# A threshold search that notes its passes in ten columns, and a scheduling clock with the trace's durations

## The chip, the cores and the metric

One core of a Trainium2 chip runs the whole program. The metric is device time in microseconds (us) of one execution. The engines named below are TensorE (PE, with its weight loads PEld), VectorE (DVE), ScalarE (ACT), GpSimd (POOL) and SyncE (SP), whose queue issues the DMAs. Each engine takes its instructions strictly in the order in which they stand in its list.

## The reference, cut to what matters

One layer of a streaming encoder runs for 2048 prompt frames and for 8 x 16 sample frames. After a common projection there are three head groups: A (causal attention with forget gates), B (attention over the best keys of an indexer) and C (attention over a band of chunks). The indexer part is what the change touches:

```python
rs = jax.nn.relu(jnp.einsum('bqhe,bke->bqhk', iq, ik) * IDX_SCALE)
score = jnp.einsum('bqh,bqhk->bqk', iw * IDX_W_SCALE, rs)
score = jnp.where(adm[None], score, -jnp.inf)
top_val, top_idx = lax.top_k(score, n_top)     # n_top = 256 for the prompt
# ... softmax attention of group B over the n_top keys of each query ...
y = x + jnp.einsum('bne,ed->bnd', g, w_out)    # g: the gated outputs of A, B and C
```

## The kernel before, in words

The work falls into streams of steps, written as Python generators: projections of the prompt (`fill_stream`, matmuls `pj<-wt,hT`), dense units of groups A and C (`maxima`, `rows`, `scores`, `products`, `end`), the indexer's scores and the choice of keys for query blocks i = 2 to 15 (`score_stream`, `select_stream`), the sample frames (`sample_stream`, tiles `yy`, `acc`, `cum`, `eq` of the selection used again), the sparse units of group B, and the output projection with the final norm (`out_stream`, matmuls `pj<-wo,gac`).

`drive` (L429) merges the streams into one program. A step says what it needs; `Clock` (L63) holds for every engine the time to which it has been given work, and for every tile when it will be ready, worked out from a cost in ns for each instruction (`Timed`, L181). `drive` gives the next piece to the stream whose need is met first; where no stream is ready, one of the fillers (projection or output matmuls) goes in. These costs therefore settle the order on PE, ACT, DVE and POOL, and nothing is reordered later. Two more decisions hang on them: `exp_split` (L514) puts the difference `Pl<-Pf` (the low half of the exponentials, which `o<-V,Pl` multiplies) on POOL or on DVE, whichever is expected free first, and every step that waits for a tile is put behind the work that is expected to be done by then.

The choice of keys, `select` (L1026), looks for a threshold with about 252 of n scores above it. A pass counts on ACT by a Sign activation over the whole row with a summed output (`eq<-acc,un`), and POOL computes from the sum the error `ee`, a changed slope `iv` (with `eg` and `hv`) and the next threshold `un`, with one element per partition. There are ten counts in a block. After `un`, POOL also keeps the best threshold so far and its count in `ub` and `eb`, with `ea` as the mark of a count that is too high. When all passes are done, DVE picks the exact set of 256 keys (among others with a prefix sum, `cum`), and the mask goes to memory as `negd`.

Three gates set the order far from the search. Block i + 1 is scored while block i is searched, since there are two `acc` tiles. `smp_stream` starts only when all 14 blocks are chosen. And `out_all` lets the output projection of the sample rows (block 16, `open_(b)` at L1987) start only when `smp_s` has ended; that is the last tile of the program.

`sample_stream` runs 24 heads, one after the other, as one list of steps: copies of the queries into `QM` (`acc<-qp`, `yy<-q`), 18 matmuls of scores, softmax on DVE and ACT, then for the head before it six transposes, four copies, 51 matmuls of products, the division on DVE, the gate on POOL, and a transpose by DMA.

A second program behind `tc.If(fv > FORCE)` is in the built lists too and is not run.

Of the kernel before, what the change touches and what calls it, by code (L numbers as in the profile page):

```python
# [10 lines left out]
F32 = mybir.dt.float32  # L11
F16 = mybir.dt.float16
BF16 = mybir.dt.bfloat16
# [22 lines left out]
TOP = 256.0  # L36
# [26 lines left out]
class Clock:  # L63
# [12 lines left out]
    @staticmethod  # L76
    def aps(args, kw):
        for x in (*args, *kw.values()):
            if hasattr(x, "tensor") and hasattr(x, "ap"):
                yield x  # L80

# [99 lines left out]
class Timed:  # L181
# [5 lines left out]
    def __getattr__(self, what):  # L187
# [3 lines left out]
        def call(*args, **kw):  # L191
# [14 lines left out]
            elif e == "DVE":  # L206
                if what == "scalar_tensor_tensor":
                    cost = (129 if ins[0].dtype == F32 and out[0].dtype == F32 and len(ins) > 2 else 68) + 1.042 * m
                elif what == "tensor_copy" and ins[0].dtype != F32:
                    cost = 68 + 0.26 * m if "ps" not in str(ins[0].tensor) else 68 + 0.52 * m  # L210
                elif what == "tensor_tensor_scan":
                    cost = 68 + 1.9 * m / 2
                else:
                    cost = 68 + 1.042 * m
            elif e == "ACT":
                cost = (52 if len(ins) == 1 else 142) + 0.836 * m + (60 if len(out) > 1 else 0)
            elif e == "POOL":
                if what == "memset":
                    cost = 40 + 0.83 * m
                elif m <= 8:  # L220
                    cost = {1: 240, 2: 260, 3: 320}.get(len(ins), 320) if what == "tensor_scalar" else 141
                else:
                    cost = 141 + 1.68 * m
# [34 lines left out]
def hybrid_step(ctx, tc, x_prompt, x_sample, cache_a_k, cache_a_v, cache_a_logf, cache_b_k, cache_b_v,  # L258
# [767 lines left out]
    def select(i, out):  # L1026
# [7 lines left out]
        def col(nm, w=1):  # L1034
            return sl.tile([128, w], F32, name=nm, bufs=2 if nm in ("ssg", "ee", "un") else 1)
# [7 lines left out]
        nmu, sa, u, iv, ub, eb = [col(k) for k in ("nmu", "sa", "u", "iv", "ub", "eb")]  # L1043
        yield need(acc, sx)
        V.reduce_sum(nmu, sx[:, :ng], axis=AX.X)
        yield need(nmu)
# [5 lines left out]
        kc = selc[:, i - 2, :]  # L1052
        G.tensor_scalar(u, kc[:, 0:1], sa, -1.0, op0=ALU.mult, op1=ALU.mult)
# [4 lines left out]
        yield need(u)  # L1058
        sums.append(sign(u))
        ep = None  # L1060
        for it in range(10):
            ss = sums.pop(0)
            yield need(ss)
            e, a = col("ee"), col("ea")
            G.tensor_scalar(e, ss, 0.5, n / 2 - TARGET, op0=ALU.mult, op1=ALU.add)
            if 0 < it < 9:
                if ep is not None:

                    g = col("eg")
                    G.tensor_scalar(g, e, ep, 0.0, op0=ALU.mult, op1=ALU.is_lt)  # L1070
                    G.tensor_scalar(iv, g, hv, iv, op0=ALU.mult, op1=ALU.add)
                ep = e
                un = col("un")
                G.tensor_scalar(un, e, iv, u, op0=ALU.mult, op1=ALU.add)
                hv = col("hv")
                G.tensor_scalar(hv, iv, -0.5, None, op0=ALU.mult)
            G.tensor_scalar(a, e, TOP - TARGET + 0.25, -1e30, op0=ALU.is_gt, op1=ALU.mult)
            if it == 0:
                G.tensor_tensor(ub, a, tiny, ALU.add)
                G.tensor_tensor(eb, a, e, ALU.add)  # L1080
                continue
            G.tensor_scalar(ub, a, u, ub, op0=ALU.add, op1=ALU.max)
            G.tensor_scalar(eb, a, e, eb, op0=ALU.add, op1=ALU.max)
            if it < 9:
                u = un
                yield need(u)
                sums.append(sign(u))
        t, m1, g, v, kk = [col(k) for k in ("tt", "m1", "gg", "vv", "kk")]
# [997 lines left out]
```

## Time and profile before

| | |
|---|---|
| median of 3 runs | 2681.66 us (2680.62 to 2687.39) |
| the profiled execution's own time | 2682.99 us |
| its span in the profile | 2681.1 us |
| busy: PE, DVE, ACT, POOL | 2403.7, 1821.8, 1383.8, 1226.5 us |
| granted TensorE clock, mean over the span | 0.972 of full speed |

The span is the time between the first and the last instruction of the profile; 1.9 us of the profiled execution lie outside it. All instructions that a helper of the scheduling clock records carry that helper's line, L192, in the profile, so groups are known by their tiles and not by their lines. A wait is idle time of an engine just before an instruction, put down to what came last.

### The profile page before, as it was taken

How to read it: one execution, taken by the hardware profiler on the slowest of the kernel's cores; microseconds unless marked ns; L12 is line 12 of the kernel's file. 1: busy time of each engine (PE TensorE's matmuls, PEld its weight loads, DVE VectorE, ACT ScalarE, POOL GpSimd, SP SyncE). 2: the span in 40 equal slices, each digit the busy share in tenths (PEclk: the TensorE clock that was granted, in tenths of full speed). 3: DMA queues.
4: the chain of work that ended last, by engine and by line, in shares of the span. 5: the costliest groups of instructions: out<-in, count | busy, mean ns of one | idle time of the engine just before them, and what ended most of it. 6: DMA issues, size and time to landing. Idle time of an engine off the chain costs nothing.

```text
span 2681.1 us, 69388 instructions
## 1 busy us (share of the span) xinstructions
PE 2403.7 (90%) x26754; PEld 1673.4 (62%) x26838; DVE 1821.8 (68%) x4865; ACT 1383.8 (52%) x2734; POOL 1226.5 (46%) x2115
## 2 busy tenths in 40 slices
PE   4997888888999899889899999957879999999998
PEld 4666666666676676667677787744546555555553
DVE  6434667788677787857857446658786676778743
ACT  6314556656665576575545344445555444443310
POOL 0014577766564375573624103426465555544300
PEclk8999999999999999999999999978899999999999
DMA  6255313233333332223354453373254333244542
GB/s 199 62 130 147 92 43 86 68 91 85 92 92 87 96 78 72 65 72 97 96 136 109 111 124 84 80 150 83 58 147 93 75 74 85 73 97 101 122 104 82
DMA packets 553190, 257.25 MB, mean 96 GB/s; under 512 B 376064, under 2 KB 541760, under 8 KB 552592
## 3 DMA queue, kind: packets, MB, share of 16 engines
q1 hardware_dynamic: 552848, 252.71, 37.7%
q8 instruction: 212, 3.47, 0.6%
q14 instruction: 130, 1.06, 0.1%
HBM read 160.37 MB, written 84.85 MB: 91 GB/s over the span
## 4 chain that ended last, share of the span: by engine, by line
PE 47%; DVE 17%; POOL 15%; issue 8%; DMA 7%; ACT 4%; SPq 1%; DVEq 0%; ACTq 0%; POOLq 0%
PE pj L192 29%; PE st L192 8%; PE o L192 5%; PE s L192 4%; POOL Pl L192 3%; DVE jk L192 3%; DVE acc L192 2%; POOL iv L192 2%; POOL un L192 2%; ACT eq L192 2%; DVE mx L192 2%; POOL eb L192 2%; POOL eg L192 1%; DVE cum L192 1%; POOL ub L192 1%
## 5 line engine op out<-in xcount | busy, mean ns | idle before, releaser
L192 POOL TENSOR_TENSOR Pl<-Pf 128x512 f16<-128x512 f32 (+3 forms) x653 | 657.4, 1017 | 584.5 <-ACT Pf L192 551.6
L192 PE MATMUL pj<-wt,hT 128*128 128x128 f16 (+1 forms) x8568 | 783.1, 244 | 5.1 <-DVE ev L192 4.0
L192 PEld LDWEIGHTS <-hT 128*128 128x128 f16 x8976 | 655.8, 98 | 126.8 <-issue 31.4
L192 ACT ACTIVATE Pf<-st,sh 128x512 f32<-128x512 f32 (+1 forms) x496 | 297.3, 612 | 284.4 <-DVE st L192 110.0
L192 PEld LDWEIGHTS <-Pf 128*128 128x128 bf16 x5472 | 315.1, 98 | 98.4 <-issue 11.2
L192 PE MATMUL pj<-hT,wt 128*128 128x512 f16 (+1 forms) x1440 | 297.1, 351 | 1.0 <-ACT yy L192 0.7
L192 PEld LDWEIGHTS <-Pl 128*128 128x128 f16 x2736 | 255.1, 99 | 53.6 <-POOL Pl L192 50.6
L192 PE MATMUL pj<-wo,gac 128*128 128x512 f16 x1224 | 284.6, 381 | 1.9 <-DVE xr L192 1.7
L192 DVE SCALAR_TENSOR_TENSOR acc<-rl,iws,acc 128x512 f32<-128x512 f32 (+3 forms) x266 | 202.3, 761 | 91.2 <-ACT rl L192 86.6
L192 ACT ACTIVATE Pf<-st,ncb 128x512 f32<-128x512 f32 (+1 forms) x320 | 192.9, 623 | 91.0 <-PE st L192 82.3
L192 PE MATMUL o<-V,Pl 128*128 128x65 f16 x1648 | 198.9, 194 | 45.3 <-POOL Pl L192 42.8
L192 DVE TENSOR_REDUCE mx<-s 128x1 f32<-128x512 f32 (+2 forms) x320 | 185.5, 603 | 75.4 <-PE s L192 73.5
L192 DVE CUSTOM_DVE_ANT_0 jk<-s,ng 128x512 bf16<-128x512 f32 (+3 forms) x304 | 188.6, 620 | 70.9 <-PE s L192 52.1
L192 ACT ACTIVATE rl<-s 128x512 f32<-128x512 f32 (+3 forms) x304 | 161.5, 543 | 136.0 <-PE s L192 72.4
L192 PE MATMUL o<-V,Pf 128*128 128x65 f16 x3296 | 219.2, 195 | 1.4 <-DVE u L192 0.8
L192 PEld LDWEIGHTS <-wt 128*128 128x128 f16 x1440 | 127.2, 99 | 127.5 <-issue 15.3
L192 PEld LDWEIGHTS <-gac 128*128 128x128 f16 x1224 | 116.8, 98 | 130.2 <-issue 5.0
L192 ACT ACTIVATE ev<-pj 128x512 f32<-128x512 f32 (+4 forms) x211 | 115.0, 545 | 148.3 <-PE pj L192 137.2
L192 ACT ACTIVATE eq<-acc,un 128x384 bf16<-128x384 f32 (+13 forms) x112 | 146.9, 1311 | 83.7 <-POOL un L192 83.3
L192 PE MATMUL st<-qp,Ka 128*128 128x512 f16 (+3 forms) x544 | 182.7, 338 | 6.5 <-ACT Pf L192 5.4
L192 PE MATMUL st<-Q,K 98*128 98x512 f16 (+3 forms) x544 | 183.4, 339 | 0.6 <-ACT Q L192 0.6
L192 DVE TENSOR_TENSOR Pl<-Pf 128x512 f16<-128x512 f32 (+3 forms) x163 | 105.6, 654 | 46.7 <-ACT Pf L192 44.9
(452 smaller groups left out, 4486.1 us busy)
## 6 DMA issues: line engine op xcount, KB each, us to landing
wst<-in_w_in SPq DMA_DIRECT2D x84, 256.0 KB
gac<-gTd SPq DMA_DIRECT2D x34, 384.0 KB
out<-ev SPq DMA_DIRECT2D x96, 128.0 KB
qTd<-ev SPq DMA_DIRECT2D x96, 128.0 KB
szd<-ev SPq DMA_DIRECT2D x96, 128.0 KB
qp<-qTd SPq DMA_DIRECT2D x96, 128.0 KB
out<-xr SPq DMA_DIRECT2D x17, 512.0 KB
xt<-in_x_prompt SPq DMA_DIRECT2D x16, 512.0 KB
```

Source lines behind the costliest of these rows:

```text
L192: r = f(*args, **kw)
```

## The change

Two things are changed. In `select`, the thresholds and the counts of the passes stand in ten columns of the tiles `us` and `es`, so that POOL only computes the error and the next threshold in a pass; the mark of counts that are too high (`am`) and the best threshold and count are taken once, at the end of a block, by five DVE instructions. And the costs of the scheduling clock are other numbers: small POOL instructions, the prefix sum, DVE and ACT instructions with a summed output, ACT instructions that read SBUF.

```diff
@@ Clock
+    @staticmethod
+    def psum(x):
+        return getattr(x.tensor, "space", DRAM) == PSUM
@@ Timed
             elif e == "DVE":
                 if what == "scalar_tensor_tensor":
-                    cost = (129 if ins[0].dtype == F32 and out[0].dtype == F32 and len(ins) > 2 else 68) + 1.042 * m
+                    cost = (129 if len(ins) > 2 else 68) + 1.042 * m
...
                 elif what == "tensor_tensor_scan":
-                    cost = 68 + 1.9 * m / 2
+                    cost = 130 + 2.09 * m
                 else:
-                    cost = 68 + 1.042 * m
+                    cost = 68 + 1.042 * m + (70 if kw.get("accum_out") is not None else 0)
             elif e == "ACT":
-                cost = (52 if len(ins) == 1 else 142) + 0.836 * m + (60 if len(out) > 1 else 0)
+                src = (ins or aps)[0]
+                cost = 52 + 0.836 * m + (0 if clock.psum(src) else 40) + (92 if len(ins) > 1 or len(out) > 1 else 0)
+                if clock.psum(src) and src.dtype == F16 and "Q" in out[0].tensor.name:
+                    cost += 134
             elif e == "POOL":
...
                 elif m <= 8:
-                    cost = {1: 240, 2: 260, 3: 320}.get(len(ins), 320) if what == "tensor_scalar" else 141
+                    cost = {1: 310, 2: 330, 3: 360}.get(len(ins), 360) if what == "tensor_scalar" else 270
                 else:
-                    cost = 141 + 1.68 * m
+                    cost = 141 + (1.68 if len(ins) < 2 or BF16 in (ins[0].dtype, ins[1].dtype) else 2.1) * m
@@ select
+        us, es, am = [col(k, 10) for k in ("us", "es", "am")]
...
+        G.memset(us[:, 0:1], -1e-30)
...
+        u = us[:, 1:2]
         G.tensor_scalar(u, kc[:, 0:1], sa, -1.0, op0=ALU.mult, op1=ALU.mult)
...
         for it in range(10):
             ss = sums.pop(0)
             yield need(ss)
-            e, a = col("ee"), col("ea")
+            e = es[:, it:it + 1]
             G.tensor_scalar(e, ss, 0.5, n / 2 - TARGET, op0=ALU.mult, op1=ALU.add)
             if 0 < it < 9:
...
-                un = col("un")
+                un = us[:, it + 1:it + 2]
                 G.tensor_scalar(un, e, iv, u, op0=ALU.mult, op1=ALU.add)
-                hv = col("hv")
-                G.tensor_scalar(hv, iv, -0.5, None, op0=ALU.mult)
-            G.tensor_scalar(a, e, TOP - TARGET + 0.25, -1e30, op0=ALU.is_gt, op1=ALU.mult)
...
-            G.tensor_scalar(ub, a, u, ub, op0=ALU.add, op1=ALU.max)
-            G.tensor_scalar(eb, a, e, eb, op0=ALU.add, op1=ALU.max)
-            if it < 9:
                 u = un
-                yield need(u)
+                if it < 8:
+                    hv = col("hv")
+                    G.tensor_scalar(hv, iv, -0.5, None, op0=ALU.mult)
+                yield need(us)
                 sums.append(sign(u))
+
+        yield need(es)
+        V.tensor_scalar(am, es, TOP - TARGET + 0.25, -1e30, op0=ALU.is_gt, op1=ALU.mult)
+        yield need(am)
+        V.tensor_tensor(us, us, am, ALU.add)
+        V.tensor_tensor(es, es, am, ALU.add)
+        yield need(us)
+        V.reduce_max(ub, us, axis=AX.X)
+        yield need(es)
+        V.reduce_max(eb, es, axis=AX.X)
+        yield need(ub, eb)
```

The built lists of the two kernels show what the new costs move. PE has the same matmuls in both lists, 26,829 without the second program, in another order. The 304th and last matmul of the indexer's scores (`s<-kiT,qi`) stands at place 11,876 before and at 13,163 now; the first matmul of the sample frames at 13,097 and now 14,430; the last of the sample frames at 26,547 and now 26,757. So 282 matmuls of the output projection stood behind the sample frames, and now 72 do, those of block 16.

POOL, one pass of the search in the last block (i = 15; `Pl` belongs to a dense unit, `mx` too), before:

```order
L192 TENSOR_TENSOR Pl<-Pf 128x512
L192 TENSOR_SCALAR ee<-ssg 128x1
L192 TENSOR_SCALAR eg<-ee 128x1
L192 TENSOR_SCALAR iv<-eg,hv,iv 128x1
L192 TENSOR_SCALAR un<-ee,iv,un 128x1
L192 TENSOR_SCALAR hv<-iv 128x1
L192 TENSOR_SCALAR ea<-ee 128x1
L192 TENSOR_SCALAR ub<-ea,un,ub 128x1
L192 TENSOR_SCALAR eb<-ea,ee,eb 128x1
L192 TENSOR_TENSOR u<-u,szl 128x256
```

Eight instructions of the search stand here behind one count, and the next work of a dense unit comes after them. A pass of the same block now:

```order
L196 TENSOR_TENSOR Pl<-Pf 128x384
L196 TENSOR_SCALAR es<-ssg 128x1
L196 TENSOR_SCALAR eg<-es 128x1
L196 TENSOR_SCALAR iv<-eg,hv,iv 128x1
L196 TENSOR_SCALAR us<-es,iv,us 128x1
L196 TENSOR_SCALAR hv<-iv 128x1
L196 TENSOR_TENSOR Pl<-Pf 128x128
```

Three instructions of a pass are gone, and the dense unit's `Pl` follows `hv` at once. Of the 816 `Pl` that are run, POOL has 653 before and 688 now.

DVE, the end of the sample frames, before (`cum,smx<-pj,eq` is the softmax's maximum of a head, `srs` and what follows it the division and gate of the head before, and `xr<-pj,xr` takes a finished output tile out of PSUM):

```order
L192 SCALAR_TENSOR_TENSOR xr<-pj,xr 128x512
L192 ISA cum,smx<-pj,eq 128x384
L192 ISA smx 128x1
L192 TENSOR_SCALAR smb<-smx 128x1
L192 TENSOR_TENSOR cum<-cum 128x384
L192 COPY acc<-pj 128x2x8x16 x2
L192 COPY acc<-pj 128x128 x2
L192 RECIPROCAL srs<-pj 128x1
L192 TENSOR_SCALAR cum<-pj,srs 128x64
L192 TENSOR_TENSOR acc<-cum,acc 128x64
L192 SCALAR_TENSOR_TENSOR xr<-pj,xr 128x512
L192 COPY acc<-pj 128x2x8x16 x2
```

An output tile is taken out ahead of the head's softmax and again behind its gate. Now, the last head and a half of the same stream:

```order
L196 TENSOR_TENSOR cum<-cum 128x384
L196 COPY acc<-pj 128x2x8x16 x2
L196 COPY acc<-pj 128x128 x2
L196 RECIPROCAL srs<-pj 128x1
L196 TENSOR_SCALAR cum<-pj,srs 128x64
L196 TENSOR_TENSOR acc<-cum,acc 128x64
L196 COPY acc<-pj 128x2x8x16 x2
L196 COPY acc<-pj 128x128 x2
L196 RECIPROCAL srs<-pj 128x1
L196 TENSOR_SCALAR cum<-pj,srs 128x64
L196 TENSOR_TENSOR acc<-cum,acc 128x64
L196 SCALAR_TENSOR_TENSOR xr<-pj,xr 128x512 x2
```

Output tiles stood between the heads; now none does in the last three heads and a half, on DVE as on PE, where the 282 matmuls of these heads (three times 18 + 6 + 51, and 6 + 51) follow each other without an output matmul between them.

SP, the end of the program before (`gTd<-yy` stores the last four sample heads, `gac<-gTd` loads one tile for the output projection, `xr<-in_x` its residual):

```order
L192 DMA_TRANSPOSE yy<-acc 128x1x128
L192 DMA xr<-in_x_prompt 128x1024
L192 DMA gTd<-yy 64x4x128 x2
L192 DMA gac<-gTd 128x12x128 x2
L192 DMA out<-xr 128x1024
L192 DMA xr<-in_x_prompt 128x1024
L192 DMA gac<-gTd 128x12x128 x2
L192 DMA out<-xr 128x1024
L192 DMA xr<-in_x_sample 128x1024
L192 DMA out<-xr 128x1024 x2
```

The `gac` load right behind `gTd<-yy` is of a prompt tile, and the one for the sample rows comes later. The end of the program now:

```order
L196 DMA out<-xr 128x1024
L196 DMA_TRANSPOSE yy<-acc 128x1x128 x4
L196 DMA gTd<-yy 64x4x128 x2
L196 DMA gac<-gTd 128x12x128 x2
L196 DMA out<-xr 128x1024
```

The last heads' transposes, the store of the sample rows and the load of the last output tile now follow each other with nothing else between.

## Rows read from the trace of the kernel before

**Rows 1.** Five stretches of the span (--windows): length in us, then busy us and count of PE, PEld, DVE, ACT and POOL, the granted clock, the DMA engines' busy share and GB/s. The choice of keys lies in the second stretch, the sample frames from the third to 2607 us.

```profile
0.00:217.00 217.00, 174.70 (x1870) 127.07 (x1871) 96.25 (x279) 86.73 (x155) 12.81 (x27) 0.94 0.50 141
217.00:1342.00 1125.00, 999.27 (x11143) 741.24 (x11143) 834.52 (x1965) 702.17 (x1370) 685.40 (x1497) 0.98 0.32 83
1342.00:1700.00 358.00, 348.48 (x4391) 273.20 (x4390) 208.94 (x613) 173.09 (x389) 103.62 (x148) 1.00 0.45 109
1700.00:2020.00 320.00, 249.89 (x3131) 164.21 (x3140) 235.71 (x550) 173.56 (x342) 154.41 (x160) 0.90 0.44 107
2020.00:2681.10 661.10, 631.35 (x6226) 367.63 (x6297) 446.36 (x1458) 248.20 (x479) 270.31 (x284) 0.99 0.38 91
```

**Rows 2.** What PE waited for between 217 and 1342 us (--waits): us in total, times, the longest.

```profile
PE s L192 <- ACT rl L192: 44.2, 41, 3.9
PE o L192 <- POOL Pl L192: 40.6, 39, 3.3
PE s L192 <- DVE mx L192: 16.9, 27, 3.0
```

**Rows 3.** The small POOL instructions of the search (--lines): count, busy us and mean ns, idle time before them.

```profile
L192 POOL TENSOR_SCALAR eb<-ea,ee,eb 128x1 f32<-128x1 f32 x126 | 55.5, 441 | 0.0
L192 POOL TENSOR_SCALAR ub<-ea,un,ub 128x1 f32<-128x1 f32 x112 | 49.5, 442 | 11.7
L192 POOL TENSOR_SCALAR ea<-ee 128x1 f32<-128x1 f32 x140 | 39.1, 279 | 9.9
L192 POOL TENSOR_SCALAR hv<-iv 128x1 f32<-128x1 f32 x112 | 28.8, 257 | 0.0
```

**Rows 4.** POOL during one pass of the last block's search (--timeline): start us, us, instruction.

```profile
1276.00 0.56 POOL L192 TENSOR_SCALAR ee<-ssg 128x1 f32<-128x1 f32 x1
...
1277.50 0.72 POOL L192 TENSOR_SCALAR un<-ee,iv,un 128x1 f32<-128x1 f32 x1
...
1279.17 0.36 POOL L192 TENSOR_SCALAR eb<-ea,ee,eb 128x1 f32<-128x1 f32 x1
...
1280.44 0.19 POOL L192 TENSOR_SCALAR ee<-ssg 128x1 f32<-128x1 f32 x1 [0.87 <-ACT eq L192]
```

**Rows 5.** What ACT waited for most between 217 and 1342 us (--waits).

```profile
ACT eq L192 <- POOL un L192: 83.3, 71, 2.5
```

**Rows 6.** DVE instructions near the new ones in size, and the prefix sum of the last block (--lines, the last one by shape).

```profile
L192 DVE TENSOR_SCALAR oh<-idx,m 128x8 f32<-128x8 f32 x14 | 4.5, 319 | 0.7 <-POOL m L192 0.7
L192 DVE TENSOR_REDUCE vv<-oh 128x1 f32<-128x8 f32 x14 | 2.1, 153 | 0.1
L192 DVE TENSOR_TENSOR_SCAN cum<-eq 128x2048 f16<-128x2048 bf16 x1 | 4.4, 4420 | 0.0
```

**Rows 7.** The steps of one sample head, from the timelines of DVE, PE and ACT; the last two rows are of the next head, where nothing lay between them.

```profile
2573.32 0.18 DVE L192 COPY yy<-q 64x128 f16<-64x128 f16 x1
2575.01 0.27 PE L192 MATMUL pj<-yy,acc 128*128 128x256 f16 x1
2577.26 0.56 DVE L192 CUSTOM_DVE_ANT_0 cum<-pj,eq 128x384 f32<-128x384 f32 x1 [3.76 <-issue]
2578.11 0.61 ACT L192 ACTIVATE cum<-cum,smb 128x384 f32<-128x384 f32 x1 [3.71 <-DVE smb L192]
2578.76 0.56 DVE L192 TENSOR_TENSOR yy<-cum 128x384 f16<-128x384 f32 x1 [0.74 <-ACT cum L192]
2579.66 0.33 PE L192 MATMUL pj<-idb,cum 128*128 128x128 bf16 x3
2580.20 0.75 DVE L192 COPY acc<-pj 128x256 bf16<-128x256 bf16 x4 [0.88 <-PE pj L192]
2582.59 1.71 PE L192 MATMUL pj<-acc 128*128 128x65 f16 x51
2584.41 0.16 DVE L192 RECIPROCAL srs<-pj 128x1 f32<-128x1 f32 x1
...
2601.23 0.17 DVE L192 RECIPROCAL srs<-pj 128x1 f32<-128x1 f32 x1 [3.38 <-PE pj L192]
2602.43 0.23 DVE L192 TENSOR_TENSOR acc<-cum,acc 128x64 f16<-128x64 f32 x1 [0.72 <-ACT acc L192]
```

**Rows 8.** DMAs of the kind that follow the last head (--timeline of SP: start of the issue, its us), and, in the last row, a stretch in which the only traffic is one `gac` load (columns as in Rows 1).

```profile
2016.87 0.92 SPq L192 DMA_DIRECT2D gTd<-gb  x2
2018.88 0.36 SPq L192 DMA_DIRECT2D gac<-gTd  x1
...
2611.19 1.34 SPq L192 DMA_TRANSPOSE yy<-acc  x1
2614.57 1.28 SPq L192 DMA_DIRECT2D gTd<-yy  x2
2637.38 1.07 SPq L192 DMA_DIRECT2D gac<-gTd  x2
2638.00:2643.00 5.00, 5.00 (x24) 2.25 (x23) 3.49 (x23) 0.72 (x2) 0.00 (x0) 1.00 0.81 157
```

**Rows 9.** PE from the last matmul of the sample frames to its end (--timeline).

```profile
2607.40 61.03 PE L192 MATMUL pj<-wo,gac 128*128 128x512 f16 x282
```

**Rows 10.** A stretch with long waits of PE in which its clock was at the lower level (--windows), and a sample head's products that fell into such a stretch (--timeline).

```profile
1757.90:1771.50 13.60, 4.83 (x28) 3.27 (x29) 2.99 (x10) 4.15 (x11) 0.00 (x0) 0.51 0.93 233
...
1775.13 3.05 PE L192 MATMUL pj<-acc 128*128 128x65 f16 x51
```

More of the change, by code (lines that the diff above doesn't have):

```diff
@@ L1034, in col @@
         def col(nm, w=1):
-            return sl.tile([128, w], F32, name=nm, bufs=2 if nm in ("ssg", "ee", "un") else 1)
+            return sl.tile([128, w], F32, name=nm, bufs=2 if nm == "ssg" else 1)
         def sign(b):
@@ L1042, in select @@
         ng = (n + 511) // 512
-        nmu, sa, u, iv, ub, eb = [col(k) for k in ("nmu", "sa", "u", "iv", "ub", "eb")]
+        nmu, sa, iv, ub, eb = [col(k) for k in ("nmu", "sa", "iv", "ub", "eb")]
+        us, es, am = [col(k, 10) for k in ("us", "es", "am")]
         yield need(acc, sx)
         V.reduce_sum(nmu, sx[:, :ng], axis=AX.X)
+        G.memset(us[:, 0:1], -1e-30)
         yield need(nmu)
@@ L1057, in select @@
         sums = [sign(tiny)]
-        yield need(u)
+        yield need(us)
         sums.append(sign(u))
-        ep = None
         for it in range(10):
@@ L1063, in select @@
             yield need(ss)
-            e, a = col("ee"), col("ea")
+            e = es[:, it:it + 1]
             G.tensor_scalar(e, ss, 0.5, n / 2 - TARGET, op0=ALU.mult, op1=ALU.add)
             if 0 < it < 9:
-                if ep is not None:
+                if it > 1:
                     g = col("eg")
-                    G.tensor_scalar(g, e, ep, 0.0, op0=ALU.mult, op1=ALU.is_lt)
+                    G.tensor_scalar(g, e, es[:, it - 1:it], 0.0, op0=ALU.mult, op1=ALU.is_lt)
                     G.tensor_scalar(iv, g, hv, iv, op0=ALU.mult, op1=ALU.add)
-                ep = e
-                un = col("un")
+                un = us[:, it + 1:it + 2]
                 G.tensor_scalar(un, e, iv, u, op0=ALU.mult, op1=ALU.add)
-                hv = col("hv")
-                G.tensor_scalar(hv, iv, -0.5, None, op0=ALU.mult)
-            G.tensor_scalar(a, e, TOP - TARGET + 0.25, -1e30, op0=ALU.is_gt, op1=ALU.mult)
[L1078 to L1081, printed above, removed]
-            G.tensor_scalar(ub, a, u, ub, op0=ALU.add, op1=ALU.max)
-            G.tensor_scalar(eb, a, e, eb, op0=ALU.add, op1=ALU.max)
-            if it < 9:
                 u = un
-                yield need(u)
+                if it < 8:
+                    hv = col("hv")
+                    G.tensor_scalar(hv, iv, -0.5, None, op0=ALU.mult)
+                yield need(us)
                 sums.append(sign(u))
+        yield need(es)
[3 more added lines that the diff above has]
+        V.tensor_tensor(es, es, am, ALU.add)
+        yield need(us)
+        V.reduce_max(ub, us, axis=AX.X)
+        yield need(es)
+        V.reduce_max(eb, es, axis=AX.X)
+        yield need(ub, eb)
         t, m1, g, v, kk = [col(k) for k in ("tt", "m1", "gg", "vv", "kk")]
```

## The prediction

> **What bounds the kernel now.** I read the busy times in stretches first. PE works 2403.7 of the 2681.1 us; the change leaves its matmuls as they are, so only the rest can change: 277 us in which PE waits, and the clock [rows 1]. PE's free time is 42 us before 217 us, 126 us in the choice of keys (1125.0 less 999.3), 10 us to 1700, 70 us to 2020 and 30 us in the last stretch, of which some 13 us follow the last matmul [rows 1, 9]. The choice of keys is thus where most is lost, at a granted clock of 0.98.
>
> The waits of that stretch come next. Three make up 102 of the 126 us: the indexer's scores wait 44.2 us for ACT's `rl` (the relu that frees their bank), the products wait 40.6 us for `Pl` from POOL, the maxima 16.9 us for DVE [rows 2]. In each of them an engine's queue, not PE, is late. Two views say why. POOL is busy 685 of 1125 us [rows 1], and in a search pass the next threshold `un` is done 2.2 us after the error was begun, but `eb` ends only 1.3 us later, at 1279.53; a `Pl` that became ready in this time would stand behind it [rows 4]. And ACT, which takes its list in order, stands 83.3 us at a Sign whose threshold POOL hasn't finished, with relus and exponentials behind it [rows 5].
>
> At the end, nothing of this kind: PE runs 282 output matmuls without a gap, 61.0 us, after the sample frames are done [rows 9]. That block of work covers everything that the last sample heads still have to do elsewhere.
>
> **The change part by part.**
>
> *Taken from POOL.* `eb`, `ub` and `ea` go with their 55.5, 49.5 and 39.1 us, and one of eight `hv`, 28.8/8 = 3.6 us: 148 us [rows 3], 22% of POOL's work in that stretch. In a pass the 1.3 us behind `un` shrink to `hv` alone, about 0.26 us [rows 3, 4]. The list shows the freed place used: 35 more `Pl` go to POOL.
>
> *Added to DVE.* Five instructions in each of 14 blocks. No row shows one on 128x10; the nearest are on 128x8, 0.32 us for an elementwise one and 0.15 for a reduction [rows 6]: 3 x 0.32 + 2 x 0.15 = 1.3 us a block, 18 us in all, from below 14 x 5 x 0.15 = 10 us. POOL's last three instructions of a block (about 1.1 us) are no longer ahead of them, but two crossings between engines come in. For the search itself this is even; DVE is busy 835 of 1125 us there [rows 1] and hides it, apart from the queue behind a DVE instruction that waits for POOL. Without that cover it would cost 18 us. `us` is one tile for all thresholds, but each is written only after the count of the one before it, so no wait is added.
>
> *The new costs, in the choice of keys.* The prefix sum takes 4.42 us for 2048 elements [rows 6]; the old cost gave it 68 + 1.9 x 1024 = 2014 ns, the new one 4410. Steps behind it were put 2.4 us too early. The small POOL instructions were below their measured 0.26 to 0.44 us [rows 3] too. With both put right, the next Sign stands later in ACT's list, with more of other work ahead of it, and ACT should not wait for POOL 71 times. What this is worth on PE can't be read off a row; the bounds are nothing and the whole 102 us. I take: of the wait for `Pl` 30 of 40.6 us, since POOL loses both the load and the 1.1 us behind which a `Pl` stood; of the wait for `rl` 24 of 44.2, since the Sign activations themselves stay in front of the relus; of the wait for DVE 4 of 16.9; and 5 us for a clock that falls less often (0.98 of 1125 us is 22 us of lower clock, some 11 us of work). Gain: 63 us, between 15 and 95.
>
> *The new costs, at the end of the program.* The search is reckoned longer, so the list spreads it over more PE work, the sample frames begin 1333 matmuls later, and their last three heads and a half have no output matmul left beside them; then come the store, the load and the 72 matmuls that need them. This is a chain with one link at a time, and its links are in the trace [rows 7]: query copies and crossings about 0.4; scores 2575.01 to 2577.26, 2.25; maximum and bias 0.85; exponential 0.65; low half 0.56 and a crossing, 0.76; transposes 0.54; copies 0.75 and a crossing, 0.85; products 1.82; division to the gated halves 2601.23 to 2602.66, 1.43. Sum 9.55 us a head. PE works about 4.0 of it (scores 2.0, transposes 0.4, products 1.6). Three heads add 3 x 5.5 = 16.6 us of waiting, the last half head (0.54 + 0.85 + 1.82 + 1.43 = 4.64, PE 1.9) 2.7 us. The DMAs add: transpose to store 3.4 us, store to load 2.0, load to landing about 5.0 (its traffic ends inside the last row) [rows 8], 10.4 us with PE idle. Sum 29.7 us. Before, the same steps lay under the 61.0 us of output matmuls [rows 9] and cost nothing.
>
> PE's clock comes on top. In the rows the granted clock is 0.51, its 1.2 GHz level, in a stretch where PE had 4.83 us of work in 13.6, and 51 products took 3.05 us there against 1.71 at 2.4 GHz [rows 7, 10]. The tail is such a stretch. If all of it ran at the lower level, PE's 13.9 us would double and the first of the 72 matmuls would be slow too, some 4 us: 18 us at most, nothing at least; I take 10. Tail: 40 us, between 27 and 50.
>
> The Trainium skill (TensorE: Matmul & The Clock Gate, "What's actually happening") says that the throttled state is the default and that activity releases it. By that rule the tail would be at 1.2 GHz throughout, and the sum 8 us higher; the trace agrees that long waits go with the lower level (0.51 in 13.6 us), but no run here yet shows the tail's bursts.
>
> *Elsewhere.* From 1342 to 2020 us the two lists run alike: the last projection matmul is at place 18,164 and now 18,010, the first output matmul at 20,699 and now 20,460. Those 80 us of waiting I leave, give or take 8.
>
> **Sum.** 2683.0 - 63 + 40 = 2660.0 us in the profiled execution's own time, which is 1.3 us above the median of the runs shown. Forecast: 2659 us.
>
> **The rivals.**
>
> 1. *The relief is nearly whole.* POOL and ACT were the only reason for the first two waits of rows 2; with POOL at some 600 of 1125 us they nearly vanish, 85 to 95 us, and the tail is the bare 30. For it: ACT's 83.3 us at POOL's thresholds [rows 5]. Against it: Sign itself stays. 2683 - 88 + 30 = 2625.
> 2. *The relief is small, the tail decides; slower.* The relus are late because ACT is full of Sign activations and exponentials and DVE of `acc` sums, and POOL's freed time goes to the 35 `Pl`. Then 15 us come back, from `Pl` alone. The place is the end of PE's list, the price 40 us, and it decides as soon as the relief is under 32 us. 2683 - 15 + 40 = 2708, or 2698 with the bare tail. For it: DVE, busy 74% there, gets more work; against it: the wait for `Pl` [rows 2] is POOL's alone.
> 3. *A wash.* The two are within 8 us of each other, the change moves waiting from the middle to the end: 2683 - 40 + 38 = 2681.
> 4. *The lower clock through the whole tail,* the mechanism of rows 10 in every burst: the tail is 48 us. 2683 - 63 + 48 = 2668. For it: PE has 4 of 9.6 us to do; against it: in the 320 us in which PE waited most, the mean granted clock was still 0.90 [rows 1].
>
> **How the numbers follow.** The forecast (2640 to 2672 about 2659) has a chance of 0.33, rival 4 0.12, rival 1 0.20, rival 2 0.21, rival 3 0.14. A measurement of this kernel tells some 0.3% (8 us) from no change: faster is the forecast with rivals 1 and 4, less a little for their edge, 0.64; same 0.15; slower 0.21. For 8 in 10 the range goes from rival 1's far side to rival 2's middle: 2615 to 2705.
>
> **What would show it.** Right: between 217 us and the end of the choice of keys, PE's wait for `Pl` is about 10 us and for `rl` about 20, and ACT's wait for a threshold is far under 83 us; small POOL instructions after `hv` are gone; after the last interleaved output matmuls there are 30 to 35 us with 282 sample matmuls, then some 10 us without any, then 72 matmuls. Wrong: waits of PE for `rl` of 40 us or more; output matmuls running up to the sample rows without a gap; a wait of DVE for the counts (`am` for `es`) that holds up `acc` sums; or PE waiting for the sample stream long before its tail.

## The result, and the profile after

The changed kernel takes 2648.5 us (median of four runs, 2647.0 to 2652.9) beside 2682.6 us for the kernel before (four runs): a ratio of 0.9873, 95% interval 0.9855 to 0.9891, so 1.3% faster. The forecast was 2659 us. The profiled execution took 2649.8 us, its span is 2648.0 us.

The list is stretched in other places than before, so I cut both traces at the same places of the program and not at the same times: the first indexer matmul, the end of the last choice on POOL, the last projection matmul, the first output matmul, the last product `o` of a dense or sparse unit, the end. First the kernel before, from the second of these stretches on without the third (columns as in [rows 1]):

```profile
211.80:1342.00 1130.20, 1002.17 (x11175) 743.10 (x11173) 836.07 (x1968) 704.40 (x1375) 685.40 (x1497) 0.98 0.32 84
...
1752.40:2032.70 280.30, 209.53 (x2521) 133.21 (x2532) 212.40 (x511) 150.48 (x295) 140.50 (x144) 0.88 0.46 111
2032.70:2528.60 495.90, 480.38 (x5157) 289.21 (x5225) 371.18 (x1151) 226.71 (x426) 256.50 (x264) 0.99 0.38 86
2528.60:2681.10 152.50, 138.93 (x909) 69.89 (x906) 65.05 (x275) 16.69 (x46) 7.07 (x12) 0.97 0.40 103
```

The kernel after, all six:

```profile
0.00:224.10 224.10, 180.41 (x1937) 133.17 (x1938) 96.00 (x280) 85.53 (x153) 12.85 (x28) 0.99 0.46 131
224.10:1374.60 1150.50, 1087.87 (x12441) 818.74 (x12439) 879.65 (x2185) 745.65 (x1471) 582.15 (x1155) 0.99 0.37 93
1374.60:1666.00 291.40, 281.22 (x3647) 215.94 (x3644) 171.67 (x456) 142.38 (x308) 100.59 (x126) 0.99 0.44 99
1666.00:1945.90 279.90, 207.30 (x2435) 131.62 (x2451) 205.88 (x508) 151.16 (x296) 138.75 (x143) 0.88 0.46 112
1945.90:2471.90 526.00, 502.99 (x5267) 299.97 (x5337) 384.64 (x1204) 235.38 (x451) 254.77 (x259) 0.99 0.40 92
2471.90:2648.00 176.10, 138.00 (x1037) 75.24 (x1034) 65.00 (x272) 21.23 (x56) 11.18 (x21) 0.89 0.29 74
```

PE's free time is length less busy. In the choice of keys it falls from 128.0 to 62.6 us, while the stretch holds 1266 more matmuls; in the last stretch it rises from 13.6 to 38.1 us. The four others together go from 135.8 to 149.5. Free time in all: 277.4 to 250.2 us, and PE's busy time falls by 5.9 us (2403.7 to 2397.8), which makes the 33.1 us of the span.

In the choice of keys, what PE waited for, then ACT's wait for a threshold, as [rows 2, 5] before:

```profile
PE s L196 <- ACT rl L196: 24.2, 34, 3.3
PE o L196 <- POOL Pl L196: 11.1, 17, 1.6
...
PE s L196 <- DVE mx L196: 6.1, 11, 1.6
...
ACT eq L196 <- POOL us L196: 38.0, 50, 1.9
```

All four are down: 44.2, 40.6, 16.9 and 83.3 us before. A pass of the search on POOL now, beside [rows 4]: behind the threshold (`us`) only `hv` is left, and a `Pl` follows it at once.

```profile
1289.10 0.19 POOL L196 TENSOR_SCALAR es<-ssg 128x1 f32<-128x1 f32 x1 [1.70 <-ACT eq L196]
...
1290.62 0.65 POOL L196 TENSOR_SCALAR us<-es,iv,us 128x1 f32<-128x1 f32 x1
1291.24 0.21 POOL L196 TENSOR_SCALAR hv<-iv 128x1 f32<-128x1 f32 x1
1291.41 1.04 POOL L196 TENSOR_TENSOR Pl<-Pf 128x512 f16<-128x512 f32 x1
```

The tail, in three windows. The first begins where no output matmul is left beside the sample heads; 282 sample matmuls and then the 72 of the sample's own block follow.

```profile
2570.60:2581.30 10.70, 4.95 (x80) 3.97 (x79) 8.08 (x36) 1.59 (x4) 1.66 (x3) 1.00 0.19 63
2581.30:2616.20 34.90, 16.76 (x207) 12.93 (x205) 7.49 (x31) 2.00 (x5) 2.29 (x5) 0.65 0.14 29
2616.20:2635.30 19.10, 18.60 (x72) 7.45 (x72) 0.71 (x2) 0.72 (x2) 0.00 (x0) 0.84 0.04 7
```

Rows of the timeline there: the products of three sample heads and of the last, and the last block, all on PE; of the second head also the first transposes on PE and the copies on DVE.

```profile
2576.35 1.86 PE L196 MATMUL pj<-acc 128*128 128x65 f16 x51 [3.21 <-DVE acc L196]
...
2584.35 0.50 PE L196 MATMUL pj<-idb,cum 128*128 128x128 bf16 x3
...
2586.54 0.75 DVE L196 COPY acc<-pj 128x256 bf16<-128x256 bf16 x4
...
2586.88 2.17 PE L196 MATMUL pj<-acc 128*128 128x65 f16 x51 [1.81 <-DVE acc L196]
...
2597.64 2.57 PE L196 MATMUL pj<-acc 128*128 128x65 f16 x51 [2.01 <-DVE acc L196]
...
2601.94 3.05 PE L196 MATMUL pj<-acc 128*128 128x65 f16 x51 [1.09 <-DVE acc L196]
2616.17 1.03 PE L196 MATMUL pj<-wo,gac 128*128 128x512 f16 x2 [11.18 <-DMA gac<-gTd]
2617.65 17.59 PE L196 MATMUL pj<-wo,gac 128*128 128x512 f16 x70 [0.45 <-DMA gac<-gTd]
```

These are 64.7 us for work that takes some 29.5 at the full clock (13.9 for the sample matmuls, by the prediction's sum, and 72 x 0.216 for the others, from 61.03 / 282 in [rows 9]). PE is free 24.4 us of it, 11.6 of them in the two waits for the last block's load, and its 40.3 us of matmul time are 10.8 more than at full speed.

### The profile page after: what moved, and what is told of

Same layout as the page of the kernel before. It is cut to its first block, busy times and chain, and to the rows that moved or that the text cites. A ratio compares the mean times of both kernels' runs of the same rounds, so it can differ in the third digit from the quotient of the medians.

```text
span 2648.0 us, 69046 instructions
## 1 busy us (share of the span) xinstructions
PE 2397.8 (91%) x26752; PEld 1674.7 (63%) x26838; DVE 1802.8 (68%) x4900; ACT 1381.3 (52%) x2734; POOL 1100.3 (42%) x1730
## 5 line engine op out<-in xcount | busy, mean ns | idle before, releaser
L196 POOL TENSOR_TENSOR Pl<-Pf 128x512 f16<-128x512 f32 (+3 forms) x688 | 683.4, 1003 | 582.2 <-ACT Pf L196 544.6
L196 PE MATMUL pj<-wo,gac 128*128 128x512 f16 x1224 | 290.5, 383 | 13.2 <-DMA gac<-gTd 11.6
L196 DVE SCALAR_TENSOR_TENSOR acc<-rl,iws,acc 128x512 f32<-128x512 f32 (+3 forms) x266 | 196.2, 738 | 87.1 <-ACT rl L196 82.5
L196 DVE TENSOR_REDUCE mx<-s 128x1 f32<-128x512 f32 (+2 forms) x320 | 185.0, 603 | 67.0 <-PE s L196 66.1
L196 PE MATMUL o<-V,Pf 128*128 128x65 f16 x3296 | 213.2, 194 | 1.0 <-ACT Pf L196 0.9
L196 PEld LDWEIGHTS <-wt 128*128 128x128 f16 x1440 | 126.3, 98 | 129.2 <-issue 13.9
L196 PEld LDWEIGHTS <-gac 128*128 128x128 f16 x1224 | 116.5, 98 | 139.5 <-DMA gac<-gTd 12.7
L196 ACT ACTIVATE eq<-acc,us 128x384 bf16<-128x384 f32 (+13 forms) x126 | 165.4, 1313 | 39.6 <-POOL us L196 38.0
L196 PE MATMUL o<-VB,Pf 128*128 128x65 f16 (+1 forms) x2176 | 132.4, 194 | 3.6 <-DVE rq_t L196 1.9
## 6 DMA issues: line engine op xcount, KB each, us to landing
out<-ev SPq DMA_DIRECT2D x96, 128.0 KB
qTd<-ev SPq DMA_DIRECT2D x96, 128.0 KB
szd<-ev SPq DMA_DIRECT2D x96, 128.0 KB
qp<-qTd SPq DMA_DIRECT2D x96, 128.0 KB
```

Source lines behind the costliest of these rows:

```text
L196: r = f(*args, **kw)
```

## The experiments

All kernels below are compared with the kernel before on the same chip; its medians there lay between 2684.2 and 2686.8 us. This table gives PE's free time in us in the six stretches named above. The traces of before and after lack some 70 matmul records in the fifth (x5157 beside x5225 weight loads), so these two numbers are some 6 us high (an estimate: 70 matmuls at the stretch's mean of 0.09 us). The expectations count PE's idle time at the end up to its last matmul, so their numbers there lie some 13 us below the table's.

| kernel | ahead | choice | to fill's end | to first output | to last `o` | end | median us | ratio (95%) |
|---|---|---|---|---|---|---|---|---|
| before | 40.0 | 128.0 | 9.5 | 70.8 | 15.5 | 13.6 | | 1 |
| after | 43.7 | 62.6 | 10.2 | 72.6 | 23.0 | 38.1 | 2648.5 | 0.9873 (0.9855 to 0.9891) |
| columns only | 39.8 | 85.0 | 19.3 | 54.3 | 15.5 | 13.7 | 2634.4 | 0.9804 (0.9788 to 0.9820) |
| costs only | 43.5 | 99.4 | 17.1 | 67.2 | 10.7 | 35.2 | 2680.6 | 0.9983 (0.9971 to 0.9995) |
| after, POOL steps put back | 43.9 | 112.3 | 9.0 | 69.7 | 18.6 | 37.6 | 2710.6 | 1.0093 (1.0078 to 1.0107) |
| after, sample forward | 42.7 | 61.5 | 28.5 | 74.9 | 20.6 | 15.8 | 2650.4 | 0.9874 (0.9860 to 0.9889) |
| after, forward from fill's end | 45.3 | 63.0 | 10.3 | 85.3 | 25.9 | 17.4 | 2642.5 | 0.9846 (0.9829 to 0.9864) |
| after, forward from output | 43.9 | 62.1 | 10.3 | 78.4 | 31.1 | 16.6 | 2643.1 | 0.9841 (0.9827 to 0.9855) |
| columns, ACT's costs | 39.6 | 91.0 | 6.7 | 55.3 | 16.5 | 14.7 | 2630.1 | 0.9784 (0.9769 to 0.9798) |
| columns, scan's cost | 40.1 | 87.3 | 16.5 | 59.1 | 15.6 | 13.6 | 2634.2 | 0.9810 (0.9791 to 0.9829) |
| columns, passes held in the list | 40.0 | 66.2 | 8.8 | 58.1 | 23.7 | 37.7 | 2644.3 | 0.9841 (0.9823 to 0.9859) |
| after, DVE's old costs | 39.4 | 65.5 | 10.6 | 66.4 | 11.0 | 21.9 | 2612.3 | 0.9725 (0.9711 to 0.9740) |
| columns, ACT's costs, no `hv` | 39.8 | 78.3 | 9.3 | 73.2 | 19.0 | 13.2 | 2637.5 | 0.9812 (0.9796 to 0.9828) |
| DVE's old costs, forward from output | 40.8 | 64.2 | 12.4 | 66.1 | 19.2 | 15.0 | 2613.4 | 0.9732 (0.9714 to 0.9749) |

**The two halves.** The new `select` with the old costs:

```diff
@@ before, select
-        nmu, sa, u, iv, ub, eb = [col(k) for k in ("nmu", "sa", "u", "iv", "ub", "eb")]
+        nmu, sa, iv, ub, eb = [col(k) for k in ("nmu", "sa", "iv", "ub", "eb")]
+        us, es, am = [col(k, 10) for k in ("us", "es", "am")]
...
```

(all of `select` as in the diff of the change, `Timed` as before).

> The columns with the clock's costs of before. In the list the search of keys then ends at 1006 us of matmul columns (before 986, after 1090), and the last sample matmul has 282 output matmuls behind it as in before (after: 72). Theory (POOL's relief is most of the gain in the choice of keys, the new costs make the uncovered tail): PE's wait for rl and Pl between 217 us and the end of the choice falls from 84.8 us to 40-55, no tail is added, 2635 to 2655 us. Rival (the gain is the new costs', which spread the search over more matmuls): the waits stay within 10 us of before and the time within 8 us of 2682. Third (both parts give half): 2655 to 2668.

And the other half, the costs of `Timed` as in the diff of the change, with the old `select`:

```diff
@@ before, Timed
-                    cost = 68 + 1.9 * m / 2
+                    cost = 130 + 2.09 * m
...
```

> The new costs with the search of before (four more POOL steps a pass). In the list the search ends at 1064 us of matmul columns, 207 sample matmuls stand behind the last of the early output blocks (after 282, before 51). Theory (POOL's relief is most of the gain): the waits for rl and Pl fall by 25 us at most, the uncovered tail of 25 to 30 us is paid, 2685 to 2710 us: slower than before. Rival (the gain is the new costs'): the waits fall by 50 us or more, 2650 to 2665 us with the tail.

Columns only, the choice of keys and the end:

```profile
211.00:1299.80 1088.80, 1003.79 (x11280) 747.32 (x11278) 840.28 (x2000) 706.14 (x1383) 557.81 (x1129) 0.98 0.34 88
2489.90:2635.40 145.50, 131.85 (x828) 65.80 (x826) 61.93 (x248) 15.60 (x43) 7.00 (x11) 0.97 0.37 101
```

Its waits in the choice of keys:

```profile
PE o L192 <- POOL Pl L192: 27.7, 29, 3.1
PE s L192 <- ACT rl L192: 27.5, 29, 3.9
...
ACT eq L192 <- POOL us L192: 47.4, 52, 2.1
```

Costs only, the same of its choice and end, then PE's wait for `rl` in its choice:

```profile
222.10:1362.30 1140.20, 1040.76 (x11760) 772.82 (x11758) 866.51 (x2043) 722.14 (x1415) 688.20 (x1487) 0.99 0.35 88
2502.00:2676.50 174.50, 139.32 (x1016) 74.53 (x1014) 67.47 (x284) 21.63 (x57) 9.72 (x19) 0.92 0.33 84
...
PE s L196 <- ACT rl L196: 33.6, 42, 2.2
```

The columns alone are 14 us faster than the whole change, and the intervals of the two ratios lie apart. They take 43 of the 65 us in the choice of keys and leave the end as it was (13.7 us). The costs alone take 29 us there, give 22 back at the end, and are 0.17% faster in all, which is within the 0.3% of no change, and not slower as I expected. Both together save more in the choice than either, and pay the tail.

**Is it POOL's load?** The kernel after, its order unchanged, with three steps in each pass whose result nobody reads and which the clock does not see:

```diff
                 G.tensor_scalar(un, e, iv, u, op0=ALU.mult, op1=ALU.add)
+                for _ in range(3):
+                    G.engine.tensor_scalar(dm, e, iv, u, op0=ALU.mult, op1=ALU.add)
```

> The kernel after, its list unchanged, with three more small POOL steps (about 360 ns each) behind each new threshold, that nobody reads and that the clock does not count: 336 steps, some 121 of the 148 us that the change took from POOL. Theory (POOL's load is what held rl and Pl up): the waits for rl and Pl rise again by 25 to 45 us, 2673 to 2695 us. Rival (the new costs' list gave the gain): within 6 us of 2648.5.

The added steps as a group (count, busy us and mean ns, idle time before them):

```profile
L1086 POOL TENSOR_SCALAR dm<-es,iv,us 128x1 f32<-128x1 f32 x336 | 134.8, 401 | 22.2
```

The choice of keys:

```profile
225.40:1442.20 1216.80, 1104.51 (x12442) 826.05 (x12441) 882.88 (x2186) 750.92 (x1471) 708.53 (x1492) 0.98 0.35 88
```

And the waits in it:

```profile
PE o L196 <- POOL Pl L196: 60.6, 57, 2.9
PE s L196 <- ACT rl L196: 21.0, 27, 3.3
...
ACT eq L196 <- POOL us L196: 83.9, 71, 2.9
```

134.8 us of POOL work cost PE 49.7 us of waiting in the choice, and 62 us of time: more than expected. PE's matmuls also take 16.6 us longer there (1104.5 us beside 1087.9), at a granted clock of 0.98 beside 0.99. So POOL's load is shown to be a cause. But the place isn't the one I had in mind: ACT waits for thresholds as long as in the kernel before (83.9 us), yet PE's wait for `rl` stays at 21.0; all of it comes back at `Pl` (11.1 to 60.6, more than the 40.6 of before; in this order POOL runs 269 `Pl` in the choice, before 208). ACT standing at a Sign thus doesn't make PE wait for relus by itself in this order. That it never does isn't shown, since a PE that waits for `Pl` also comes to its relus later.

**Can the tail be won back?** The sample stream is let forward in the list, from its start, from the end of the fill (the projections' matmuls), and from the output on:

```diff
-    smp_s = Stream(smp_stream(), 300.0)
+    smp_s = Stream(smp_stream(), -600.0)
@@ the second
-    smp_s = Stream(smp_stream(), 300.0)
+    smp_s = Late(smp_stream(), 300.0)
+    class Late(Stream):
+        def at(self):
+            self.slack = -1000.0 if (not fill_s.live) else 300.0
+            return Stream.at(self)
```

The third has `len(ended) >= na and aw_done` as its condition and -1500.

> The kernel after with the sample heads let forward in the list: the slack that the program gives their stream is -600 ns instead of 300, so the list takes a sample step up to 0.6 us before its operands are due. The last sample matmul then has 198 output matmuls behind it (after: 72, of which 70 wait for the sample's own block). Theory (the tail of 65 us holds 29.5 us of work at full pace and the rest is uncovered chain and transfers): 25 to 35 us less, 2613 to 2624 us, and PE busy 0.9 or more to its end. Rival (what the tail loses is only moved: PE waits at the sample steps earlier instead): 2635 to 2650 us.

> The kernel after; the sample stream's slack is -1000 ns, but only once the fill (the projections' matmuls) is over, 300 before. 228 output matmuls stand behind the last sample matmul. Theory (the tail's 25 us of idle PE are free to win, and what the run with the sample forward from the start lost, it lost before the end of the fill, where PE's idle time rose by 18 us): PE idle after the last product of the sparse heads falls from 25 to under 5 us, the rest stays within 5 us, 2622 to 2632 us. Rival (whatever the sample gains at the end is paid at its earlier steps): idle between the end of the fill and the sparse heads' end rises by 15 us or more, 2640 to 2655 us.

> The same with -1500 ns, only from where the output matmuls may begin; 180 output matmuls stand behind the last sample matmul. Theory: as the run with -1000 from the fill's end, 2622 to 2634 us. Rival: 2640 to 2655 us.

First variant, up to the fill's end, and the end; then the third variant from the output on:

```profile
1370.10:1688.50 318.40, 289.88 (x3684) 219.47 (x3682) 174.40 (x469) 148.56 (x323) 101.90 (x127) 0.98 0.41 95
2499.90:2645.80 145.90, 130.15 (x884) 66.52 (x882) 63.19 (x263) 20.61 (x55) 7.50 (x14) 0.96 0.38 98
```

```profile
1956.00:2486.30 530.30, 499.23 (x5311) 296.66 (x5310) 386.39 (x1216) 231.44 (x441) 257.18 (x263) 0.99 0.38 87
2486.30:2641.20 154.90, 138.33 (x964) 70.88 (x960) 63.69 (x267) 21.27 (x58) 7.99 (x15) 0.97 0.36 97
```

The rival is right in the first: the end loses 22 us of free time, and the stretch before the fill's end gains 18. In the other two a gain is left, but it is 6 us, not 20, and the intervals of their ratios still touch that of the change: the end wins some 21 us, and between the fill's end and the last `o` 14 to 16 us come in (some 20, if the missing records of after are counted in). A sample head put forward makes PE wait for its own operands: in the second, PE's wait for `qi`, which holds the sample stream's keys there, is 41.5 us up to the first output matmul where the change has 28.3; in the third, its wait for `acc`, which holds their products' operands, from there to the last `o` is 14.6 us beside 4.4.

**Which cost does it?** Columns with ACT's new costs alone, and with the scan's alone:

```diff
@@ columns only, Timed, first kernel
-                cost = (52 if len(ins) == 1 else 142) + 0.836 * m + (60 if len(out) > 1 else 0)
+                src = (ins or aps)[0]
+                cost = 52 + 0.836 * m + (0 if clock.psum(src) else 40) + (92 if len(ins) > 1 or len(out) > 1 else 0)
...
@@ columns only, Timed, second kernel
-                    cost = 68 + 1.9 * m / 2
+                    cost = 130 + 2.09 * m
```

> Columns with the clock's costs of before but for ACT's, which are the new ones (a Sign with its sum 0.836 ns an element and 184 ns, a Relu or Exp from PSUM 52). The list's search ends at 1006 us as in the columns alone, 150 output matmuls stand behind the last sample matmul. Theory of the prediction (the later Sign in ACT's list gives the relief at rl): PE's idle time in the choice of keys falls from 84.8 us (columns alone) to 60-70, no tail, 2612 to 2624 us. Rival (the spread of the search over more matmuls, which this list does not have, gives it): idle 80 us or more, 2630 to 2642 us.

> Columns with the costs of before but for the scan's, 130 + 2.09 ns an element instead of 68 + 0.95. The list's search ends at 1017 us (columns alone 1006), no tail (282 output matmuls behind the last sample matmul). Theory of the prediction (the scan's right cost spreads the selections and gives a part of the relief): idle in the choice of keys 70 to 80 us, 2622 to 2632 us. Rival (nothing by itself): within 5 us of 2634.

Neither does anything in the choice of keys (91.0 and 87.3 us beside 85.0): both expectations of mine fell, and both rivals came true. POOL's new costs alone were not run. Next, a spread without any true cost, and the change without DVE's costs:

```diff
@@ columns only, select
-            yield need(ss)
+            yield Need(lambda: clock.at(ss) + 1800.0)
@@ after, Timed
-                    cost = (129 if len(ins) > 2 else 68) + 1.042 * m
+                    cost = (129 if ins[0].dtype == F32 and out[0].dtype == F32 and len(ins) > 2 else 68) + 1.042 * m
-                    cost = 68 + 1.042 * m + (70 if kw.get("accum_out") is not None else 0)
+                    cost = 68 + 1.042 * m
```

> Columns with the costs of before; in the list each pass of the search is held 1.8 us longer behind its count (on the chip nothing waits longer, only the order of issue differs). The list's search then ends at 1076 us of matmul columns (columns alone 1006, after 1090), 72 output matmuls stand behind the last sample matmul and 282 sample matmuls behind the last early output block, both as after. Theory (what the new costs did was to spread the search over more matmuls, for better in the choice of keys and for worse at the end, and it matters little which cost did it): PE idle 60 to 70 us in the choice of keys (columns alone 84.8, after 61.9), 22 to 28 us at the end (0.9, 25.3), 2640 to 2655 us. Rival (the costs' truth counts, each engine's steps standing where they are due): idle 80 us or more in the choice, 2655 to 2670 us.

> The kernel after with one group of costs as before: DVE's products with a sum (68 instead of 129 ns and no 70 ns for a sum). The list's search ends at 1039 us of matmul columns, 84 output matmuls stand behind the last sample matmul and only 51 sample matmuls behind the last early output block (after: 72 and 282). Theory (spread and tail come together): idle 72 to 80 us in the choice, 3 to 12 us at the end (the last block's transfers of some 11 us), 2632 to 2642 us. Rival (DVE's cost is what the choice gained by): idle 85 us or more in the choice, 2640 to 2650 us.

The spread kernel's choice and end:

```profile
212.10:1376.70 1164.60, 1098.44 (x12506) 824.93 (x12504) 888.47 (x2173) 749.80 (x1475) 590.57 (x1176) 0.99 0.35 91
2454.60:2645.20 190.60, 152.95 (x1122) 83.10 (x1119) 73.46 (x304) 23.86 (x63) 12.64 (x24) 0.89 0.32 83
```

The choice and the end of the kernel with DVE's old costs:

```profile
209.60:1305.80 1096.20, 1030.70 (x11733) 770.04 (x11731) 847.02 (x2052) 720.45 (x1413) 574.46 (x1113) 0.99 0.36 90
2450.70:2608.30 157.60, 135.74 (x959) 70.34 (x957) 65.73 (x275) 21.38 (x58) 7.89 (x15) 0.95 0.36 93
```

Its last block's first matmuls in PE's timeline:

```profile
2577.11 1.03 PE L196 MATMUL pj<-wo,gac 128*128 128x512 f16 x2 [7.37 <-DMA gac<-gTd]
```

The false delay does what the new costs do, in both places: 66.2 us in the choice, 37.7 at the end, 2644.3 us in all. So spreading the search over more matmuls is enough for both; the costs need not be nearer to the durations for it. The other kernel is the best of all, 36 us faster than the change. It has the small wait in the choice (65.5) at half the spread, which I did not expect, so the spread is not all that counts there; its sample heads are covered, and of the tail little more than the last block's load is left. The end wins 16 of its 36 us; the rest lies in stretches that this edit doesn't aim at, and no run says why. At the end the free time goes with the spread as long as the sample stream isn't moved: with the list's search ending at 986 (before), 1006, 1017, 1039, 1064, 1076 and 1090 us of matmul columns, PE is free 13.6, 13.7, 13.6, 21.9, 35.2, 37.7 and 38.1 us there. Why ACT's, the scan's and POOL's costs together reach 65 us where ACT's and the scan's alone reach nothing isn't settled; it may be POOL's.

**One step less.** On the kernel with columns and ACT's costs:

```diff
-                    G.tensor_scalar(g, e, es[:, it - 1:it], 0.0, op0=ALU.mult, op1=ALU.is_lt)
-                    G.tensor_scalar(iv, g, hv, iv, op0=ALU.mult, op1=ALU.add)
+                    G.tensor_scalar(g, e, es[:, it - 1:it], 0.0, op0=ALU.mult, op1=ALU.is_ge)
+                    G.tensor_scalar(iv, g, 0.5, iv, op0=ALU.max, op1=ALU.mult)
-                    hv = col("hv")
-                    G.tensor_scalar(hv, iv, -0.5, None, op0=ALU.mult)
```

> Columns and ACT's new cost (2630 us), and one POOL step a pass less: the halved step width hv goes, the sign test becomes 'not below zero' and the width is multiplied by the larger of it and 0.5, which gives the same numbers. 98 of the POOL steps (some 310 ns each, 30 us) are gone; the list's search ends at 994 us of matmul columns, 294 output matmuls stand behind the last sample matmul. Theory (each POOL step in the search costs PE: 336 steps put back cost 49 us of idle and 62 us of time): idle in the choice falls from 89.8 by 10 to 16 us, 2610 to 2622 us. Rival (what is left at rl and Pl does not hang on POOL's load any more, or the search standing closer in the list takes it back): idle 85 us or more, 2625 to 2635 us.

The free time in the choice falls by 12.7 us for 98 steps, as expected, 0.13 us a step beside 0.15 in the kernel with 336 put back. But the time is 7 us longer and not 8 to 20 shorter as expected: from the fill's end to the first output matmul PE is free 73.2 us instead of 55.3. Nearly all of that is its wait for `qi`, the sample stream's keys: 27.4 us instead of 10.4 (28.3 in the change, 9.4 with the columns alone). In that stretch the kernels whose sample stream isn't moved lie between 54 and 73 us without any of them touching it on purpose, and what decides how late these keys are is not shown.

**The best kernel with the sample forward** (as the third variant, with -600):

> The kernel with DVE's old cost (2612 us), with the sample stream's slack at -600 ns from where the output matmuls may begin. 198 output matmuls stand behind the last sample matmul (84 without it). Theory (its end still waits 9 us, most of them for the sample's own block through DRAM, and here the sample is nearly in time, so little is paid for it): idle at the end under 2 us, elsewhere within 4 us, 2602 to 2609 us. Rival (as in the two runs before that let the sample forward: what the end gains PE waits for at earlier sample steps): 2610 to 2620 us.

The end goes from 21.9 to 15.0 us, and the stretch to the last `o` from 11.0 to 19.2. Same time, 2613.4: the rival again. Here PE's new waits are small ones for several tiles (no single one grows by over 2.5 us), so that they are for the sample's operands isn't shown.

## Why the prediction was right, and where not

*Where PE's time is lost, and that POOL holds it there.* Right for `Pl`. For the choice of keys 58 us of waits (and 5 of clock) were forecast, and 65.4 us of free time went: `Pl` by 29.5 us (forecast 30), `rl` by 20 (24), `mx` by 10.8 (4). Putting POOL's steps back shows the cause at `Pl`. The way to `rl`, over ACT's wait for thresholds [rows 5], is not borne out: that wait fell by more than half as forecast, and came back without `rl` following. So that `rl` fell by nearly what was forecast is in part luck. How its fall divides between columns and costs can't be said: each alone lowers it (to 27.5 with the columns, 33.6 with the costs), and a PE that waits at one place gives the other time.

*What the costs do there.* This step failed in its reason. I put the gain down to two costs set right, the scan's and POOL's small steps, by which the next Sign stands later. The scan's alone gave nothing, and the false delay gave as much as all the true costs; POOL's alone stay untested. Most of the gain is POOL's relief (43 of 65 us without any new cost).

*DVE's five instructions.* Forecast 1.3 us a block and hidden.

```profile
L196 DVE TENSOR_TENSOR us<-us,am 128x10 f32<-128x10 f32 x14 | 5.3, 377 | 0.2
...
L196 DVE TENSOR_SCALAR am<-es 128x10 f32<-128x10 f32 x14 | 4.5, 324 | 1.1 <-POOL es L196 0.9
...
L196 DVE TENSOR_TENSOR es<-es,am 128x10 f32<-128x10 f32 x14 | 2.2, 160 | 0.0
...
L196 DVE TENSOR_REDUCE ub<-us 128x1 f32<-128x10 f32 x14 | 2.1, 152 | 0.0
L196 DVE TENSOR_REDUCE eb<-es 128x1 f32<-128x10 f32 x14 | 2.1, 152 | 0.0
```

1.2 us a block, 16.2 us in all, and 0.9 us of waiting for the last count: nothing is held up.

*The tail.* Right in place and size: 64.7 - 29.5 = 35.2 us, forecast 40 (27 to 50). The sum of the steps had 29.7 us of waiting and 10 for the granted clock; the rows show 24.4 and 10.8. The DMAs took 11.6 (forecast 10.4). The heads' own waiting is 12.8 us instead of 19.3. The sum put steps one behind the other that lie side by side here: the transposes, which are of the head before, stand right behind the scores, beside the softmax (2584.35), and the products begin 0.34 us after the copies, while these still run (2586.54, 2586.88). PE's own steps are longer at the lower clock, so the products of the heads follow each other by 10.5 and 10.8 us all the same, where the steps of [rows 7] summed to 9.55. The two halves show that the tail is the costs' alone, and the spread kernel that a list in which the search ends nearly as late (1076 beside 1090 us) brings it without them.

The granted clock was 1.00 in the tail's first 10.7 us, 0.65 in the next 34.9, 0.84 in the last 19.1; it fell after the first head, in which PE had waited 3.2 and 2.0 us. The Trainium skill (TensorE: Matmul & The Clock Gate, "What's actually happening") says that the throttled state is the default and that activity releases it; by my reading, in which bursts like these don't release it, the whole tail would have stood at 1.2 GHz and cost 48 us. The trace agrees that waits go with the lower level (0.65), not that the bursts all ran at it.

*The granted clock in the choice.* This term was mis-sized: 5 us were taken, out of 22 us of lower clock. With only two levels, a mean of 0.98 over 1125 us is some 45 us at the lower one. Laid against the trace's clock records, PE worked 39.3 us at the lower level in this stretch before and 16.2 after, which is worth some 11 us (an estimate, at half the speed). The choice thus gave some 77 us, where 63 were forecast.

*Elsewhere.* Forecast 0, give or take 8. The four other stretches lose 13.7 us of free time: 3.7 ahead of the search, which now begins 12 us later, 0.7, 1.8 and 7.5. PE's busy time is 5.9 us less although the tail's clock adds 10.8, so the other matmuls took some 17 us less. Some 11 of these are the choice's clock; ahead of the search, PE's work at the lower level falls from 13.7 to 3.4 us, worth some 5, and up to the fill's end it rises from 0 to 6.1; the rest I can't place. The stretch ahead of the search had a mean clock between 0.94 and 1.00 in the other kernels, so chance may be in it.

The sum in the profile: -65.4 + 24.5 + 13.7 - 5.9 = -33.1, forecast -23. The choice gave 14 us more than taken and the tail cost 5 us less, and some 9 us are lost elsewhere, at the edge of the 8 allowed. That the forecast is only 10.5 us high is therefore luck in part.

*The rivals.* That the relief is small and the tail decides has no support: 65 us, where it decides below 32. That the relief is nearly whole isn't it either (35.3 us at `rl` and `Pl` are left). A wash isn't it (34 us faster), nor is the lower clock through the whole tail (35 us of loss, not 48). A slower kernel did come out where POOL had its steps back and the tail stayed, by 0.9%.

## What to carry to other kernels

Take small steps off an engine that others wait for, and measure it by putting a known number back that the scheduling clock doesn't count: here a POOL step of 0.4 us cost PE about 0.15 us. A cost table that sets the order is tried one group at a time: nearer to the durations was 14 us worse than the old table with the same columns, and one group less was 22 us better than it. And look at what runs out at the end of a list when something in the middle is spread, since letting the late part forward here mostly moved its waits.

## What the runs showed that I had not expected

Small POOL steps of one element per partition take very different times: in the kernel after, `es<-ssg` takes 229 ns, `hv<-iv` 274, `us<-es,iv,us` 594.

```profile
L196 POOL TENSOR_SCALAR us<-es,iv,us 128x1 f32<-128x1 f32 x112 | 66.5, 594 | 11.3
...
L196 POOL TENSOR_SCALAR es<-ssg 128x1 f32<-128x1 f32 x140 | 32.1, 229 | 118.0 <-ACT eq L196 116.6 <-PE st L196 0.6
L196 POOL TENSOR_SCALAR hv<-iv 128x1 f32<-128x1 f32 x98 | 26.8, 274 | 0.0
```

The scheduling clock's new 310 to 360 ns for them are too high for the first two and too low for the third. What they read is not the whole of it: the same step with an output that nobody reads, `dm<-es,iv,us`, took 401 ns. Whether it is the wait for the step just before isn't shown.
